# A hybrid decoder layer on one core: first unit in three pieces, products of zeros ahead of it, six buffers for rows of x, two roots through ACT

## The chip, the cores and the metric

The kernel runs on one core of one Trainium2 chip. A core has TensorE (PE, matrix products; PEld is its weight load), VectorE (DVE), ScalarE (ACT), GpSimd (POOL) and SyncE (SP, which here only issues DMAs), and 16 DMA engines that all queues share. The metric is device time in microseconds (us), the median of several runs.

## The reference

One decoder layer (DEPTH = 1) on 256 tokens and 16 learned meta tokens, 2048 wide, in float32:

```python
h = _rmsnorm(h_res, norm_mix_g[l])
proj = h @ w_in[l]                       # q 1024 | k 256 | v 256 | u 1024
q = _rmsnorm(q, q_norm_g[l]); k = _rmsnorm(k, k_norm_g[l])
attn = _sliding_window_attention(q, k, v, attn_sinks[l])    # 16 heads, 4 KV heads, window 128
ssm = _s5_mixer(u, ...)                  # 64 groups x 16 channels, complex state of 64, GELU, GLU
mix = concatenate([_rmsnorm(attn, ...), _rmsnorm(ssm, ...)])
h_res = h_res + mix @ w_out[l]
h2 = _rmsnorm(h_res, norm_mlp_g[l])
h_res = h_res + jnp.square(jax.nn.relu(h2 @ w_up[l])) @ w_down[l]
return h_res[:, N_META:]
```

`_rmsnorm` divides each row by the root of its mean square plus 1e-6.

## The kernel before

Weights come in units of 512 KB: 4 k-tiles of 128 rows by 256 columns (`cols`) or 2 by 512 (`rows`). `run` lists all units in `self.plan`; `unit` issues loads ahead (`load`), prepares the next ones (`part`) and hands one over. Most weights are split into a rounded part `hi` (ACT) and the rest `lo` (DVE), and a product is made of three fast ones (`mm3`). The first two phases, u0 and k0 (`RAW = 2`, eight units), are *whole*: the raw weights go into full float32 products, each recorded as two PE instructions. The operand of these phases is x transposed (`xT`, laid out by the host with the meta tokens first), 4 tiles of 4 k-tiles by 272 tokens. Tile `c` is loaded beside unit `c` of u0 by `load_xT`, on SP's queue, and scaled by the norm's weight on ACT by `split_xT`, one k-tile at a time. `split_hT` makes the rounded pair `hTh`, `hTl` of it for the phases after. The order of the phases is u0, k0, v0, q0, u1, q1, u2, u3 (`ORDER`), then the output projection, the gate and the MLP. u0's products run over two halves of 128 columns, each over the unit's four k-tiles.

The norm's divisor per token is applied late: `load_x` brings the rows of x in six pieces (two halves of 128 tokens, of the next 128, and of the 16 meta tokens), into buffers `xn` that hold 3 at a time; `token_rstd` squares and sums them on ACT and calls `rsqrt`, which makes the inverse root by an integer trick and three Newton steps on DVE (12 small operations). The result is spread over the partitions by small products (`rb`) and multiplied into k, v and u. `k_norm` calls `rsqrt` again for the heads of k. These six loads, and that of the state-space matrices `bc`, are issued by SP just before the last unit of k0.

Beside the projections run two generators, attention (`att`) and state space (`ssm`). `step`, after each unit, feeds them while a planner's clocks for DVE and ACT are less than a lead (1.5 us at first) ahead of the planner's clock for PE. That clock starts at 5.7 us for the first unit (`split_xT`). A scheduler then orders each engine's queue by priority and its own timing; on the chip each queue runs in that order.

`constants` sets up small tables at the start: a tile of zeros (DVE; `WARM = 0` products use it), the identity, the masks `m8`, `gm`, `blk2`, slopes (POOL). The five large tiles of the state-space operators (`Vr`, `Vi`, `Wr`, `Wn`, `MT`, each 128 x 1024) are cleared by POOL in `ssm_in(0)`.

Of the kernel before, what the change touches and what calls it, by code (L numbers as in the profile page):

```python
# [8 lines left out]
F32 = mybir.dt.float32  # L9
F32R = mybir.dt.float32r  # L10
I32 = mybir.dt.int32
AF = mybir.ActivationFunctionType
ALU = mybir.AluOpType
AX = mybir.AxisListType
MULT, ADD, SUB, MAX, MIN = ALU.mult, ALU.add, ALU.subtract, ALU.max, ALU.min

P = 128
D = 2048
# [6 lines left out]
HD = 64  # L25
SW = 1024
FF = 8192
EPS = 1e-6
NKT = D // P
CT = 4  # L30
# [22 lines left out]
RAW = 2  # L53
XROWS = (3, 2, 6)
BC = 3
HALVES = 1
WARM = 0
PTV, PMV, AOV = (3,), False, True
LEAD = (1.5, 3.0, 6.0, 1.0, 6.0)
PRICE = (1.0, 1.2, 1.0)  # L60
# [42 lines left out]
class Trunk:  # L103
    def __init__(self, tc, ins, out, dbg=None):
        self.tc = tc
        self.nc = PacedCore(tc.nc)
        self.clock = self.nc.clock
        self.i = ins
        self.out = out
        self.dbg = dbg or {}  # L110
        self.ssm, self.att, self.evac = [], [], []
        self.spent = {}
        self.rows_x, self.squared = [], []
        self.norms = iter(())
        self.halves = 1
        self.share, self.lead = 0.5, 1.5
        self.late = None
        self.plan, self.raws, self.units, self.when = [], {}, {}, {}
        self.nd = self.ns = self.nu = 0
# [72 lines left out]
            return self.ms2.tile([P, 512], F32, tag="ms2", name=name[1:])  # L192
        return self.ms.tile([P, 512], F32, tag="ms", name=name)

    def rsqrt(self, pool, y, ss, n, name, rows=P):

        sh = list(ss.shape)
        v = pool.tile(sh, F32, tag="rs_v", name=f"rv_{name}")
        self.ts(v, ss, 1.0 / n, MULT, EPS, ADD)
        ti = pool.tile(sh, I32, tag="rs_i", name=f"ri_{name}")  # L200
        self.nc.vector.tensor_scalar(ti, v.bitcast(I32), 1, None, op0=ALU.logical_shift_right)
        self.nc.vector.tensor_scalar(y.bitcast(I32), ti, -1.0, 1597463007.0, op0=MULT, op1=ADD)
        t = pool.tile(sh, F32, tag="rs_t", name=f"rt_{name}")
        for _ in range(3):
            self.tt(t, y, y, MULT)
            self.stt(t, t, -0.5, v, MULT, MULT)
            self.stt(y, t, 1.5, y, ADD, MULT)

    def load(self):
        n = self.nd  # L210
        dram, k0, nk, c0, ncol, first, _, whole = self.plan[n]
        tag = ("hi", "lo", "raw")[n % 3] if whole else "raw"
        raw = self.ring.tile([P, nk, ncol], F32, tag=tag, bufs=3, name=f"raw{n}")
        m = nk // HALVES if n == 0 else nk
        for k in range(0, nk, m):
            if first:
                first(k, m)
            self.nc.sync.dma_start(out=raw[:, k:k + m, :], in_=dram[(k0 + k) * P:(k0 + k + m) * P, c0:c0 + ncol].rearrange("(k p) c -> p k c", p=P))
        self.raws[n] = raw
        self.nd += 1  # L220
# [111 lines left out]
    def constants(self):  # L332
        nc, c = self.nc, self.cst

        w = self.st.tile([P, D // 2], F32, tag="xn", bufs=3, name="zeros")[:, 0:256]
        nc.vector.memset(w, 0.0)
        wp = self.ps("warm")
        for _ in range(WARM):
            nc.tensor.matmul(wp[:, 0:256], lhsT=w[:, 0:P], rhs=w, start=True, stop=True)
        g = nc.gpsimd  # L340
        self.ones = c.tile([P, 1], F32, name="ones")
        g.memset(self.ones, 1.0)

        nc.scalar.activation(c.tile([P, 1], F32, name="early"), self.ones, AF.Copy)
        self.ident = c.tile([P, P], F32, name="ident")
        make_identity(nc, self.ident)
        m8 = c.tile([P, 8], F32, name="m8")
        g.memset(m8, 1.0)
        g.affine_select(out=m8, in_=m8, pattern=[[-16, 8]], compare_op=ALU.is_ge, fill=0.0, base=0, channel_multiplier=1)
        g.affine_select(out=m8, in_=m8, pattern=[[16, 8]], compare_op=ALU.is_ge, fill=0.0, base=15, channel_multiplier=-1)  # L350
        self.m8 = m8
        self.gm = c.tile([P, 2], F32, name="gm")
        nc.vector.tensor_reduce(out=self.gm, in_=m8.rearrange("p (k x) -> p x k", x=2), axis=AX.X, op=ADD)
        self.blk2 = c.tile([P, 2], F32, name="blk2")
        nc.vector.tensor_reduce(out=self.blk2, in_=m8.rearrange("p (x k) -> p x k", x=2), axis=AX.X, op=ADD)
        self.slope = c.tile([P, 2, NH], F32, name="slope")
        self.qsc = c.tile([P, NH], F32, name="qsc")
        for h in range(NH):
            g.memset(self.slope[:, :, h:h + 1], -SLOPES[h])
            g.memset(self.qsc[:, h:h + 1], HD ** -0.5 / SLOPES[h])  # L360
# [39 lines left out]
    def load_xT(self, c, k, m):  # L400

        if k == 0:
            self.xT[c] = self.st.tile([P, 4, L], F32, tag="xT", bufs=4, name=f"xT{c}")
        r = 512 * c + P * k
        self.nc.sync.dma_start(out=self.xT[c][:, k:k + m, :], in_=self.i["xT"][r:r + P * m, :].rearrange("(k p) t -> p k t", p=P))

    def split_xT(self, c):

        t = self.xT[c]
        for k in range(4):  # L410
            kt = 4 * c + k
            self.nc.scalar.activation(t[:, k, :], t[:, k, :], AF.Copy, scale=self.g_in[:, kt:kt + 1])
        self.clock["t"] = max(self.clock["t"], 5.7 + 3.7 * c)

    def split_hT(self, c):
        for k in range(2):
# [4 lines left out]

    def load_x(self, n):

        k, h = n // 2, n % 2
        src = self.i["meta_tokens"] if k == 2 else self.i["x"][0][k * P:k * P + P, :]
        t = self.st.tile([P, D // 2], F32, tag="xn", bufs=3, name=f"x{k}{h}")[0:src.shape[0], :]
        self.nc.sync.dma_start(out=t, in_=src[:, h * (D // 2):(h + 1) * (D // 2)])
        self.rows_x.append(t)

    def token_rstd(self):  # L430

        nc = self.nc
        s2 = self.cst.tile([P, 3, 2], F32, name="s2x")
        ss = self.cst.tile([P, 3], F32, name="ss")
        nc.gpsimd.memset(s2, 1.0)
        for n in range(6):
            while n >= len(self.rows_x):
                yield
            t = self.rows_x[n]
            nc.scalar.activation(t, t, AF.Square, accum_out=s2[0:t.shape[0], n // 2, n % 2:n % 2 + 1])  # L440
            self.squared.append(n)
            yield
        nc.vector.tensor_reduce(out=ss, in_=s2, axis=AX.X, op=ADD)
        self.rs_x = self.cst.tile([P, 3], F32, name="rs_x")
        self.rsqrt(self.cst, self.rs_x, ss, D, "x")
        yield
        self.rb = self.asm.tile([P, L], F32, name="rb")
        rp = self.ps("rb")
        for k, (n, o) in enumerate(((P, NM), (P, NM + P), (NM, 0))):
            rr = self.KT[:, k, 0:P]  # L450
            nc.vector.tensor_copy(rr, self.rs_x[:, k:k + 1].to_broadcast([P, P]))
            nc.tensor.matmul(rp[:, o:o + n], lhsT=rr[0:n, :], rhs=self.ident[0:n, 0:n], start=True, stop=True)
        nc.vector.tensor_copy(self.rb, rp[:, 0:L])
        yield
# [172 lines left out]
    def ssm_in(self, Q):  # L627

        nc = self.nc
        if Q == 0:  # L630
            nc.gpsimd.tensor_scalar(self.C[1], self.C[1], -1.0, None, op0=MULT)
        if Q == 0:
            self.ops = [self.spb.tile([P, 8, CT, 2, 16], F32, name=nm) for nm in ("Vr", "Vi", "Wr", "Wn")]
            self.MT = self.spb.tile([P, 8, P], F32, name="MT")
            for z in self.ops + [self.MT]:
                nc.gpsimd.memset(z, 0.0)
        Vr, Vi = self.ops[0:2]
        (br, bi) = self.B
        yield from self.prod(Q, Vr, br, bi, self.Fr, self.Fi, SUB)
        yield from self.prod(Q, Vi, br, bi, self.Fi, self.Fr, ADD)  # L640
# [218 lines left out]
    def k_norm(self, kr):  # L859
        nc = self.nc  # L860
        NT, TW = 4, 68
# [5 lines left out]
        sp = self.ps("kss").rearrange("p (k n) -> p k n", n=4)  # L867
# [1 line left out]
            for i in range(2):  # L869
                nc.tensor.matmul(sp[0:TW, t, 2 * i:2 * i + 2], lhsT=sq[i][:, t * TW:t * TW + TW], rhs=self.blk2, start=True, stop=True)  # L870
        rk = self.atp.tile([TW, NT, 4], F32, name="rk")
        self.rsqrt(self.atp, rk, sp[0:TW, 0:NT, :], HD, "k")
        yield
        rbs = [self.ps(f"krb{i}")[:, 0:L] for i in range(2)]
        for t in range(NT):
# [203 lines left out]
    def run(self):  # L1079
# [22 lines left out]
        self.Vm = self.asm.tile([P, 2, 4, HD], F32, name="Vm")  # L1102
        self.qT = self.asm.tile([P, 8, NX], F32, name="qT")
        self.U = self.spd.tile([P, NPAIR, NCH], F32, name="U")
        self.grp, self.xT, self.ready = {}, {}, set()
        w_in, w_glu, w_out, w_up, w_down = (i[n][0] for n in ("w_in", "w_glu", "w_out", "w_up", "w_down"))
        tk = [slice(NM, NM + P), slice(NM + P, NM + 2 * P)]
        xt = [slice(0, P), slice(P, 2 * P)]

        self.cols(w_in, 1536, NKT, [lambda k, m, c=c: self.load_xT(c, k, m) for c in range(4)], [lambda c=c: self.split_xT(c) for c in range(4)], True)  # L1110
        loads = {BC: lambda k, m: nc.sync.dma_start(out=self.bc, in_=i["ssm_bc"])}
        for n in range(6):
            k = XROWS[0] + (n >= XROWS[2]) * (n - XROWS[2] + 1)
# [227 lines left out]
```

## Time and profile before

| | |
|---|---|
| median of 3 runs | 1065.33 us (1064.19 to 1066.98) |
| profiled run | 1063.85 us, its span 1062.1 us |
| PE busy | 1043.9 us, 98% of the span |
| DVE, ACT, POOL busy | 677.0, 517.8, 10.3 us |
| DMA | 192.07 MB, mean 181 GB/s |
| first product on PE | 7.22 us after the span's start |

A row of the timeline gives start, duration, engine, line, operation, tiles (out<-in), shapes and count (xN: N of them merged) and, in brackets, the idle time before it and what ended it. SPq rows are issues of DMAs. A row of waits gives the total, the count and the longest. Since all operations pass through helpers, most lines read L80 or L81; the tiles' names tell the place.

### The profile page before, as it was taken

Reading aid. Unit: us, or ns where it says so; the run is one execution under the profiler, and the core shown is the slowest. Engines: PE = TensorE matmul, PEld = TensorE weight load, DVE = VectorE, ACT = ScalarE, POOL = GpSimd, SP = SyncE. Lnnn points to the kernel's source line nnn. Section 1 sums busy time; section 2 is a strip of 40 time slices with the busy share of each in tenths; the row PEclk is TensorE's granted clock in tenths of the full one; section 3 lists DMA queues with packets and bytes.
Section 4 is the critical chain, followed back from the end, with each engine's and each line's share of the span. In section 5 each row is a group of like instructions: output and inputs, shape, how many; then the busy total and the mean of one; then the engine's idle time right before and its main releaser. Section 6 shows DMA issues by size and latency. Waiting matters only on the chain.

```text
span 1062.1 us, 14956 instructions
## 1 busy us (share of the span) xinstructions
PE 1043.9 (98%) x5724; PEld 896.5 (84%) x5724; DVE 677.0 (64%) x1121; ACT 517.8 (49%) x742; POOL 10.3 (1%) x62
## 2 busy tenths in 40 slices
PE   7999999999999999999999999999999999999998
PEld 5879788878998888888888888888888888888886
DVE  8988887739586766554556655456565555665553
ACT  6744768454475645433344543335444334544332
POOL 3000000000000000000000000000000000000000
PEclk9999999999999999999999999999999999999999
DMA  9563534155565666666666666666665666666673
GB/s 332 164 180 101 168 100 128 43 168 176 177 191 172 184 190 185 191 197 190 191 194 184 193 192 193 192 198 184 193 192 186 196 195 186 194 192 184 216 212 127
DMA packets 145929, 192.07 MB, mean 181 GB/s; under 512 B 9632, under 2 KB 97824, under 8 KB 145472
## 3 DMA queue, kind: packets, MB, share of 16 engines
q1 hardware_dynamic: 145856, 191.10, 58.3%
q8 instruction: 45, 0.74, 0.3%
q14 instruction: 28, 0.23, 0.1%
HBM read 186.03 MB, written 4.26 MB: 179 GB/s over the span
## 4 chain that ended last, share of the span: by engine, by line
PE 92%; DVE 4%; ACT 2%; issue 1%; DMA 1%; SPq 0%; ACTq 0%; DVEq 0%
PE up L81 34%; PE dn L81 33%; PE wb L81 4%; PE q L81 4%; PE u L81 4%; PE wt L81 3%; PE y L80 2%; PE g L81 2%; PE pv L80 2%; PE s L80 1%; DVE room L81 1%; PE z L80 1%; DVE gt L81 1%; DVE lo L80 1%; DMA xT<-in_xT 1%
## 5 line engine op out<-in xcount | busy, mean ns | idle before, releaser
L80 DVE TENSOR_TENSOR lo<-raw,hi 128x1024 fp32r<-128x1024 f32 x328 | 401.3, 1224 | 291.0 <-ACT hi L80 290.5
L80 ACT ACTIVATE hi<-raw 128x1024 fp32r<-128x1024 f32 x328 | 347.5, 1060 | 378.2 <-PE dn L81 199.5
L81 PE MATMUL up<-h,hi 128*128 128x512 f32 x1024 | 245.5, 391 | 0.0
L81 PEld LDWEIGHTS up<-h,hi 128*128 128x128 f32 x1024 | 188.0, 188 | 36.3
L81 PE MATMUL dn<-lo,ah 128*128 128x512 f32 x512 | 199.2, 389 | 0.0
L81 PE MATMUL dn<-hi,al 128*128 128x512 f32 x512 | 199.2, 389 | 0.0
L81 PE MATMUL dn<-hi,ah 128*128 128x512 f32 x512 | 178.4, 389 | 0.0
L81 PEld LDWEIGHTS up<-h,lo 128*128 128x128 f32 x1024 | 131.5, 191 | 5.1
L81 PE MATMUL up<-h,lo 128*128 128x256 f32 x1024 | 133.2, 283 | 0.0
L81 PEld LDWEIGHTS dn<-hi,ah 128*128 128x128 f32 x512 | 96.1, 188 | 20.0
L81 PEld LDWEIGHTS dn<-lo,ah 128*128 128x128 f32 x512 | 96.1, 188 | 19.9
L81 PEld LDWEIGHTS dn<-hi,al 128*128 128x128 f32 x512 | 96.1, 188 | 19.9
L81 ACT ACTIVATE r<-up 128x256 f32<-128x256 f32 x64 | 23.9, 373 | 56.4 <-PE up L81 56.4
L81 DVE TENSOR_TENSOR r<-up,r 128x256 f32<-128x256 f32 x64 | 27.0, 421 | 29.3 <-ACT r L81 29.3
L81 PE MATMUL wt<-hi,ma 128*128 128x512 f32 x128 | 40.5, 395 | 1.5 <-ACT ma L81 1.4
L81 PEld LDWEIGHTS wt<-hi,ma 128*128 128x128 f32 x128 | 23.7, 188 | 7.0 <-ACT ma L81 1.8
L81 PE MATMUL u<-hTh,lo 128*128 128x272 f32 x96 | 28.7, 301 | 0.0
L81 PE MATMUL u<-hTh,hi 128*128 128x272 f32 x96 | 28.5, 299 | 0.0
L81 PE MATMUL u<-hTl,hi 128*128 128x272 f32 x96 | 28.2, 294 | 0.0
L81 ACT ACTIVATE ah<-s 128x512 fp32r<-128x512 f32 x32 | 20.2, 630 | 15.2 <-DVE s L81 15.2
L81 PE MATMUL q<-lo,hTh 128*128 128x512 f32 x64 | 26.0, 407 | 0.8 <-DVE lo L80 0.8
L81 PE MATMUL wt<-lo,ma 128*128 128x512 f32 x64 | 25.1, 395 | 0.9 <-DVE lo L80 0.9
(289 smaller groups left out, 1161.8 us busy)
## 6 DMA issues: line engine op xcount, KB each, us to landing
raw<-in_w_up SPq DMA_DIRECT2D x128, 512.0 KB, 3.9
raw<-in_w_down SPq DMA_DIRECT2D x128, 512.0 KB, 4.1
raw<-in_w_in SPq DMA_DIRECT2D x40, 512.0 KB, 4.1
raw<-in_w_out SPq DMA_DIRECT2D x32, 512.0 KB, 4.0
raw<-in_w_glu SPq DMA_DIRECT2D x8, 512.0 KB, 4.3
xT<-in_xT SPq DMA_DIRECT2D x4, 544.0 KB, 7.4
x<-in_x SPq DMA_DIRECT2D x4, 512.0 KB, 10.2
xm<-in_x SPq DMA_DIRECT2D x2, 1024.0 KB, 6.2
```

Source lines behind the costliest of these rows:

```text
L80: return f(*args, **kw)
L81: return f(*args, **kw)
```

## The change

- `FIRST = ((0, 1), (1, 1), (2, 2))`: unit 0's weights and its `xT` tile are loaded in three pieces, of one, one and two k-tiles. The weights' pieces stay on SP's queue; those of `xT` tile 0 go to ACT's queue, ahead of ACT's first operation.
- `WARM = 4`: PE first multiplies zeros, four products of 256 columns.
- The buffers `xn` become six; the rows of the meta tokens are loaded first. The scratch for dynamic DMAs is set to 2048 bytes.
- `rsqrt` gets a second form for x and k: ACT's Sqrt (on the mean plus epsilon), DVE's reciprocal and one Newton step. ACT's first operation becomes a Sqrt.
- The five large tiles are cleared at the start, four by POOL and `Vr` by DVE; the two reductions of `m8` into `gm` and `blk2` move from the start to `ssm_in(0)`.
- The planner's PE clock starts at 4.0 instead of 5.7 us.

```diff
-HALVES = 1
-WARM = 0
+FIRST = ((0, 1), (1, 1), (2, 2))
+WARM = 4
...
-    def rsqrt(self, pool, y, ss, n, name, rows=P):
+    def rsqrt(self, pool, y, ss, n, name, table=False):
...
+        t = pool.tile(sh, F32, tag="rs_t", name=f"rt_{name}")
+        if table:
+            self.nc.scalar.activation(t, ss, AF.Sqrt, scale=1.0 / n, bias=self.eps[0:sh[0], :])
         self.ts(v, ss, 1.0 / n, MULT, EPS, ADD)
-        ti = pool.tile(sh, I32, tag="rs_i", name=f"ri_{name}")
...
-        for _ in range(3):
+        if table:
+            self.nc.vector.reciprocal(y, t)
+        else:
+            ti = pool.tile(sh, I32, tag="rs_i", name=f"ri_{name}")
...
+        for _ in range(1 if table else 3):
...
-        m = nk // HALVES if n == 0 else nk
-        for k in range(0, nk, m):
+        for k, m in FIRST if n == 0 else ((0, nk),):
...
-        w = self.st.tile([P, D // 2], F32, tag="xn", bufs=3, name="zeros")[:, 0:256]
+        w = self.st.tile([P, D // 2], F32, tag="xn", bufs=6, name="zeros")[:, 0:256]
...
-        nc.scalar.activation(c.tile([P, 1], F32, name="early"), self.ones, AF.Copy)
+        self.eps = c.tile([P, 1], F32, name="eps")
+        g.memset(self.eps, EPS)
+
+        self.ops = [self.spb.tile([P, 8, CT, 2, 16], F32, name=nm) for nm in ("Vr", "Vi", "Wr", "Wn")]
+        self.MT = self.spb.tile([P, 8, P], F32, name="MT")
+        nc.vector.memset(self.ops[0], 0.0)
+        for z in self.ops[1:] + [self.MT]:
+            g.memset(z, 0.0)
+        for k, m in FIRST:
+            self.load_xT(0, k, m)
+
+        nc.scalar.activation(c.tile([P, 1], F32, name="early"), self.ones, AF.Sqrt)
...
-        nc.vector.tensor_reduce(out=self.gm, in_=m8.rearrange("p (k x) -> p x k", x=2), axis=AX.X, op=ADD)
...
-        self.nc.sync.dma_start(out=self.xT[c][:, k:k + m, :], in_=...)
+        (self.nc.sync if c else self.nc.scalar).dma_start(out=self.xT[c][:, k:k + m, :], in_=...)
...
-        self.clock["t"] = max(self.clock["t"], 5.7 + 3.7 * c)
+        self.clock["t"] = max(self.clock["t"], 4.0 + 3.7 * c)
...
-        k, h = n // 2, n % 2
+        k, h = (n // 2 + 2) % 3, n % 2
...
-        self.rsqrt(self.cst, self.rs_x, ss, D, "x")
+        self.rsqrt(self.cst, self.rs_x, ss, D, "x", True)
...
-            for z in self.ops + [self.MT]:
-                nc.gpsimd.memset(z, 0.0)
+            nc.vector.tensor_reduce(out=self.gm, ...)
+            nc.vector.tensor_reduce(out=self.blk2, ...)
...
-        self.rsqrt(self.atp, rk, sp[0:TW, 0:NT, :], HD, "k")
+        self.rsqrt(self.atp, rk, sp[0:TW, 0:NT, :], HD, "k", True)
...
-    nc = bacc.Bacc("TRN2", target_bir_lowering=False, num_devices=1)
+    nc = bacc.Bacc("TRN2", target_bir_lowering=False, num_devices=1, dynamic_dma_scratch_size=2048)
```

More of the change, by code (lines that the diff above doesn't have):

```diff
@@ L112, in __init__ @@
         self.spent = {}
-        self.rows_x, self.squared = [], []
+        self.rows_x, self.squared, self.xT = [], [], {}
         self.norms = iter(())
@@ L193, in ps @@
         return self.ms.tile([P, 512], F32, tag="ms", name=name)
-    def rsqrt(self, pool, y, ss, n, name, rows=P):
+    def rsqrt(self, pool, y, ss, n, name, table=False):
         sh = list(ss.shape)
         v = pool.tile(sh, F32, tag="rs_v", name=f"rv_{name}")
+        t = pool.tile(sh, F32, tag="rs_t", name=f"rt_{name}")
+        if table:
+            self.nc.scalar.activation(t, ss, AF.Sqrt, scale=1.0 / n, bias=self.eps[0:sh[0], :])
         self.ts(v, ss, 1.0 / n, MULT, EPS, ADD)
-        ti = pool.tile(sh, I32, tag="rs_i", name=f"ri_{name}")
-        self.nc.vector.tensor_scalar(ti, v.bitcast(I32), 1, None, op0=ALU.logical_shift_right)
-        self.nc.vector.tensor_scalar(y.bitcast(I32), ti, -1.0, 1597463007.0, op0=MULT, op1=ADD)
-        t = pool.tile(sh, F32, tag="rs_t", name=f"rt_{name}")
-        for _ in range(3):
+        if table:
+            self.nc.vector.reciprocal(y, t)
+        else:
+            ti = pool.tile(sh, I32, tag="rs_i", name=f"ri_{name}")
+            self.nc.vector.tensor_scalar(ti, v.bitcast(I32), 1, None, op0=ALU.logical_shift_right)
+            self.nc.vector.tensor_scalar(y.bitcast(I32), ti, -1.0, 1597463007.0, op0=MULT, op1=ADD)
+        for _ in range(1 if table else 3):
             self.tt(t, y, y, MULT)
@@ L352, in constants @@
         self.gm = c.tile([P, 2], F32, name="gm")
-        nc.vector.tensor_reduce(out=self.gm, in_=m8.rearrange("p (k x) -> p x k", x=2), axis=AX.X, op=ADD)
         self.blk2 = c.tile([P, 2], F32, name="blk2")
-        nc.vector.tensor_reduce(out=self.blk2, in_=m8.rearrange("p (x k) -> p x k", x=2), axis=AX.X, op=ADD)
         self.slope = c.tile([P, 2, NH], F32, name="slope")
@@ L404, in load_xT @@
         r = 512 * c + P * k
-        self.nc.sync.dma_start(out=self.xT[c][:, k:k + m, :], in_=self.i["xT"][r:r + P * m, :].rearrange("(k p) t -> p k t", p=P))
+        (self.nc.sync if c else self.nc.scalar).dma_start(out=self.xT[c][:, k:k + m, :], in_=self.i["xT"][r:r + P * m, :].rearrange("(k p) t -> p k t", p=P))
     def split_xT(self, c):
@@ L422, in load_x @@
     def load_x(self, n):
-        k, h = n // 2, n % 2
+        k, h = (n // 2 + 2) % 3, n % 2
         src = self.i["meta_tokens"] if k == 2 else self.i["x"][0][k * P:k * P + P, :]
-        t = self.st.tile([P, D // 2], F32, tag="xn", bufs=3, name=f"x{k}{h}")[0:src.shape[0], :]
+        t = self.st.tile([P, D // 2], F32, tag="xn", bufs=6, name=f"x{k}{h}")[0:src.shape[0], :]
         self.nc.sync.dma_start(out=t, in_=src[:, h * (D // 2):(h + 1) * (D // 2)])
@@ L439, in token_rstd @@
             t = self.rows_x[n]
-            nc.scalar.activation(t, t, AF.Square, accum_out=s2[0:t.shape[0], n // 2, n % 2:n % 2 + 1])
+            nc.scalar.activation(t, t, AF.Square, accum_out=s2[0:t.shape[0], (n // 2 + 2) % 3, n % 2:n % 2 + 1])
             self.squared.append(n)
@@ L632, in ssm_in @@
         if Q == 0:
-            self.ops = [self.spb.tile([P, 8, CT, 2, 16], F32, name=nm) for nm in ("Vr", "Vi", "Wr", "Wn")]
-            self.MT = self.spb.tile([P, 8, P], F32, name="MT")
-            for z in self.ops + [self.MT]:
-                nc.gpsimd.memset(z, 0.0)
+            nc.vector.tensor_reduce(out=self.gm, in_=self.m8.rearrange("p (k x) -> p x k", x=2), axis=AX.X, op=ADD)
+            nc.vector.tensor_reduce(out=self.blk2, in_=self.m8.rearrange("p (x k) -> p x k", x=2), axis=AX.X, op=ADD)
         Vr, Vi = self.ops[0:2]
@@ L1104, in run @@
         self.U = self.spd.tile([P, NPAIR, NCH], F32, name="U")
-        self.grp, self.xT, self.ready = {}, {}, set()
+        self.grp, self.ready = {}, set()
         w_in, w_glu, w_out, w_up, w_down = (i[n][0] for n in ("w_in", "w_glu", "w_out", "w_up", "w_down"))
@@ L1108, in run @@
         xt = [slice(0, P), slice(P, 2 * P)]
-        self.cols(w_in, 1536, NKT, [lambda k, m, c=c: self.load_xT(c, k, m) for c in range(4)], [lambda c=c: self.split_xT(c) for c in range(4)], True)
+        self.cols(w_in, 1536, NKT, [None] + [lambda k, m, c=c: self.load_xT(c, k, m) for c in range(1, 4)], [lambda c=c: self.split_xT(c) for c in range(4)], True)
         loads = {BC: lambda k, m: nc.sync.dma_start(out=self.bc, in_=i["ssm_bc"])}
```

## The prediction

> **What bounds the kernel now.** I read the page first (engine totals), then PE's waits, then the work by stage, then the chain and the timeline where the change acts.
>
> ```profile
> PE 1043.9 (98%) x5724; PEld 896.5 (84%) x5724; DVE 677.0 (64%) x1121; ACT 517.8 (49%) x742; POOL 10.3 (1%) x62
> ```
> ```profile
> PE u L81 <- DMA raw<-in_w_in: 7.2, 1, 7.2
> PE kss L80 <- ACT ksq L81: 1.4, 1, 1.4
> PE wt L81 <- ACT ma L81: 1.4, 1, 1.4
> PE wt L81 <- DVE lo L80: 0.9, 1, 0.9
> PE z L80 <- DMA U<-du: 0.9, 1, 0.9
> PE q L81 <- DVE lo L80: 0.8, 1, 0.8
> PE v L81 <- ACT qT L81: 0.6, 1, 0.6
> PE vti L80 <- ACT VTr L81: 0.5, 1, 0.5
> ```
>
> PE is the bound: 98% of the span, and its waits add up to 13.7 us, 7.2 of them before its first product. A microsecond saved ahead of a stage in which PE never waits is kept to the end. The stages (stretch, its length, busy time of PE, PEld, DVE, ACT, POOL; last columns clock, DMA share, GB/s):
>
> ```profile
> 7.00:24.30 17.30, 17.08 (x65) 13.84 (x66) 16.93 (x106) 11.20 (x24) 2.88 (x11) 1.00 1.09 367
> 24.30:32.00 7.70, 7.70 (x35) 6.41 (x34) 7.56 (x32) 5.17 (x10) 0.84 (x1) 1.00 1.04 364
> 40.00:65.00 25.00, 21.61 (x162) 19.16 (x162) 24.14 (x66) 14.10 (x25) 0.00 (x0) 1.00 0.50 142
> 90.00:210.00 120.00, 120.00 (x862) 104.70 (x860) 96.59 (x254) 77.25 (x181) 0.23 (x2) 1.00 0.38 113
> ```
>
> So PE decides, except that from 7 to 65 us DVE is full as well, and 40 to 65 is where PE waits for DVE and ACT. Whatever PE gains at the front must be followed by DVE there, or the wait at 64 grows.
>
> **1. The first unit.** Now it is one transfer of x^T (544 KB) and one of weights (512 KB), behind the vectors (101 KB), all from SP.
>
> ```profile
> raw<-in_w_in SPq DMA_DIRECT2D x40, 512.0 KB, 4.1
> ...
> xT<-in_xT SPq DMA_DIRECT2D x4, 544.0 KB, 7.4
> ...
> vecs<-in_vecs SPq DMA_DIRECT2D x1, 101.0 KB, 2.1
> ```
> ```profile
> 0.92 0.27 DVE L81 MEMSET zeros<- 128x256 f32 x1 [0.92 <-PEq L1331]
> ...
> 1.25 0.42 SPq L405 DMA_DIRECT2D xT<-in_xT  x1
> ...
> 5.65 1.76 ACT L81 ACTIVATE xT<-xT,vecs 128x272 f32<-128x272 f32 x4 [3.36 <-DMA xT<-in_xT]
> ...
> 8.25 2.48 PE L81 MATMUL u<-xT,raw 128*128 128x272 f32 x5
> 11.43 2.03 PE L81 MATMUL u<-xT,raw 128*128 128x272 f32 x7
> 15.82 4.52 PE L81 MATMUL u<-xT,raw 128*128 128x272 f32 x19
> 24.30 8.41 PE L81 MATMUL k<-xT,raw 128*128 128x272 f32 x36
> ```
> ```profile
> L81 PE MATMUL u<-xT,raw x64: 392/392/791, 7.2 to 24.1; 128*128 128x272 f32 x64
> ```
> ```profile
> 0.00:3.00 3.00, 0.00 (x0) 0.00 (x0) 0.62 (x5) 1.49 (x2) 2.37 (x46) 1.00 0.32 57
> 3.00:4.00 1.00, 0.00 (x0) 0.00 (x0) 1.00 (x5) 0.00 (x0) 1.00 (x2) 1.00 0.95 306
> 4.00:5.00 1.00, 0.00 (x0) 0.00 (x0) 1.00 (x5) 0.00 (x0) 1.00 (x2) 1.00 1.06 360
> 5.00:6.00 1.00, 0.00 (x0) 0.00 (x0) 1.00 (x5) 0.35 (x1) 1.00 (x2) 1.00 1.10 386
> ```
>
> Early products start some 0.45 us apart (the five of the row from 8.25 less a last one of 0.65: 1.83 over four steps); later ones 0.229 ((4.52 - 0.39) / 18). The fast spacing sets in at about 11.4, so PE runs at half pace for its first 4.2 us, though the granted clock reads 1.00. The 64 instructions of u0 take 24.3 - 7.2 = 17.1 us; at 0.229 they would take 14.7.
>
> After: four products of zeros, two instructions each, 256 columns: 8 x 0.45 x 256/272 = 3.4 us from about 1.25 (the zeros are cleared by 1.19; PE's queue runs in order, so they are in the way until they end) to 4.7. The first two pieces (x^T 136 KB and weights 128 KB each) can be there by then: with the vectors 629 KB, which the four window rows pass at 4.5 us, less 0.45 for the issue of x^T that leaves SP's queue; ACT's scaling is 0.5 us a piece (1.76 for four, overlapped). The third piece holds half the unit. All 1157 KB (1.18 MB) had moved at 5.9 us by these rows (0.17 + 0.31 + 0.36 + 0.39), the weights had landed at 7.2, 1.3 later. With 0.45 saved the third piece lands near 6.8. So: k-tiles 0 and 1 from 4.7 to about 5.9, a pause to 6.8, tiles 2 and 3 to 7.75 (ACT's pace), the second half of the columns 4 x 0.45 = 1.8 to 9.55, three more units of 16 x 0.229 = 3.66: u0 ends at 20.55 instead of 24.3. Gain 3.75. ACT gives up some 1.2 us for three issues (0.4 each, by SP's rows), before it has anything to scale. Bounds: all in time, 4.7 + 14.7 = 19.4, gain 4.9; nothing sooner and no clock, gain 0.
>
> "TensorE: Matmul & The Clock Gate" of the Trainium skill (Part 1, What's actually happening) says that full clock follows a busy window of 3.4 us which runs freely, so 3.4 to 6.8 us after the first product. The 4.2 us here agree; by the late end (estimate from that page) full clock would come at 8.1 and the gain would be 1.4 us smaller. "DMA: Bandwidth & Descriptors" (Issuing engines are not separate DMA queues) says a second issuing queue saves only issue time; that is how I counted it, and were the two queues to share bandwidth unluckily the third piece would land at 7.2 as before and cost 0.4 of the gain.
>
> **2. Clearing moves.** Four operators go from POOL at 2.9 us to POOL at its start, the fifth to DVE.
>
> ```profile
> 2.88 0.96 POOL L636 MEMSET Vr<- 128x1024 f32 x1
> 6.44 0.95 POOL L636 MEMSET MT<- 128x1024 f32 x1
> 2.88 4.54 DVE L81 TENSOR_SCALAR vecs<-vecs 128x16 f32<-128x16 f32 x1 [0.61 <-DMA vecs<-in_vecs]
> 7.47 0.23 DVE L81 TENSOR_SCALAR room<-vecs 128x32 f32<-128x32 f32 x1
> ```
>
> DVE's first operation lasts exactly as long as POOL's five clears (2.88 to 7.39): it is held by them, and DVE really begins at 7.47. After, four clears of 0.89 from about 0.85 end at 4.4; POOL's small work that stood before them (2.1 of the 2.37 us up to 3.0) follows, to 6.5. DVE's own clear (about 1.1, four times the 0.27 for 256 columns) falls into time in which it has nothing. DVE begins between 4.4 and 6.5: 1 to 3 us sooner; I take 1.5, since many small POOL operations follow the long ones. The two reductions of m8, moved later, cost DVE about 0.2.
>
> **3. Six buffers for the rows of x.**
>
> ```profile
> SPq L427 <- ACT x L81: 6.9, 3, 4.2
> ```
> ```profile
> DVE ss L81 <- ACT x L81: 0.8, 1, 0.8
> ```
> ```profile
> L81 ACT ACTIVATE x<-x x6: 1042/1057/1057, 24.9 to 41.4; 128x1024 f32<-128x1024 f32 x4, 16x1024 f32<-16x1024 f32 x2
> ```
> ```profile
> bc<-in_ssm_bc SPq DMA_DIRECT2D x1, 1024.0 KB, 10.0
> ```
>
> With three buffers SP's queue waited 6.9 us for squares. Now all six go in a row, ahead of the last weights of k0. The squares (1.06 + 0.19 each) reach from 24.9 to 42.6, up to where PE's waits of 0.5 and 0.6 stand on ACT (VTr, qT); they can move into ACT's idle time of 7 to 32 us (17.3 - 11.20 + 7.7 - 5.17 = 8.6); DVE's wait of 0.8 goes. PE arrives 3.75 sooner, so I count 0.6 of the 1.1 (bounds 0 and 1.1). Price: k0's last weights stand behind 101 + 4 x 1056 + 3 x 512 + 1024 + 2176 KB, with their own 512 KB 9.8 MB: 1.22 by 6 us, the rest at 365 GB/s, is 29.5, landed 30.8. PE needs them at 20.55 + 3 x 3.66 = 31.5. It just fits; I take 0.2 (bounds 0 and 1.5).
>
> **4. Roots.** Twelve small DVE operations become five, for x and for k.
>
> ```profile
> L81 DVE SCALAR_TENSOR_TENSOR rs_x<-rt_x,rs_x x3: 142/145/155, 47.4 to 55.4; 128x3 f32<-128x3 f32 x3
> ```
>
> Seven fewer at about 0.1 us of queue time each (0.145 long, and such operations overlap): 0.7 for x. k's lie behind the wait for ksq and are covered by q's products; without that cover they would be worth the same again. The last of x's steps stands at 55.4, 13 us after the last square, because each waits its turn between other work; five turns and one hop to ACT should be over sooner. ACT loads a table before its first operation in either kernel, and k's root comes before the first exponential and the first Gelu, so no load is added.
>
> **5. The wait at 61 to 64 (0.8 + 1.4).** DVE must reach the products with rb sooner by as much as PE does (3.75 + 0.6 - 0.2 = 4.15). It has 1.5 (clears) + 0.8 (wait) + 0.7 - 0.2 (roots, reductions) = 2.8, and the planner's PE clock for the first unit falls from 5.7 to 4.0, so up to 1.7 us less state-space work is put ahead: 4.5. I leave the wait as it is: 0 (bounds: 2.2 worse, 2.2 better).
>
> **Sum.** 3.75 + 0.6 - 0.2 + 0 = 4.15, say 4.2 us. The profiled run took 1063.85 (span 1062.1 and 1.75 around it); the median of the three runs, 1065.33, is 1.5 above. Against the median: 1061.1.
>
> **Rivals.**
> *DVE follows only half way.* POOL's whole start holds it to 6.5 and the planner's shift does not help: 2.3 (1.0 + 0.8 + 0.5) where 4.15 are needed, the wait at 64 grows by 1.9, gain 2.3: 1063.0. For it: DVE's 24.14 of 25 busy. Against: ACT's and SP's waits go too.
> *The zeros come late.* If POOL's clears hold DVE's clear of the zeros as they hold the 4.54 us operation, the zero products run from 4.5 to 7.9, real ones follow, fast from 8.7 (two of 64 done by then): u0 ends near 22.9, gain 1.4: 1063.9. Against: "SBUF — State Buffer" (Who interferes with whom) of the Trainium skill exempts a DVE operation with at most one SBUF input outside the two-port modes; no row here shows a clear beside a long one.
> *Slower: the state-space tail comes out of its cover.*
>
> ```profile
> 279.33 2.82 PE wt L81 x12
> 282.15 6.56 PE g L81 x55
> ```
>
> These are rows of the chain: only 2.8 us of products separate the last y, which ends at 279.3, from g, which needs its results through two transfers. Less state-space work early (the planner's 1.7) shifts it later; once the tail is over 4.2 us later against PE, PE's idle time there exceeds the gain; at 8 us the time is 1065.3 - 4.2 + 8 = 1069. Against: DVE has 23 us free from 90 to 210.
>
> **How the numbers follow.** Forecast (gain 3.2 and more) 0.62; DVE half way 0.18; zeros late or nothing sooner 0.12; slower 0.08. 0.3% is 3.2 us, about what a measurement of this kernel can tell from no change: faster 0.62, within 0.3% 0.30, slower 0.08. Best case 4.9 + 1.1 + 2.2 = 8.2; the forecast's own range is 1057.1 to 1062.1. The range takes in the two small gains, the second down to 0.3 us: 1057.0 to 1065.0; slower is left out.
>
> **What would show it.** Right: zero products from 1.3, real ones from 4.7, k0 at about 20.5 instead of 24.30; DVE's first long operation over by 4.4 to 6.5; no SP wait on squares; the root of x before 50; q's wait for ksq not above 1.4. Wrong: first real product after 7, spacing of 0.45 beyond 9 us, waits at 60 to 65 above 4, or a gap between y and g at 270 to 280.

## The result, and the profile after

The changed kernel takes 1057.43 us (median of 4 runs, 1056.99 to 1058.02), the kernel before 1064.76 on the same chip: a ratio of 0.993 (95% interval 0.9918 to 0.9942). The profiled run took 1057.23 us with a span of 1055.5, against 1063.85 and 1062.1. So 6.6 us went out of the span, where 4.2 were forecast; the medians differ by 7.3, and 1057.43 lies 0.4 above the lower end of the predicted range.

The page's engine totals and PE's waits over the whole span, changed kernel (total, count, longest):

```profile
PE 1045.0 (99%) x5732; PEld 897.0 (85%) x5732; DVE 671.6 (64%) x1108; ACT 519.4 (49%) x744; POOL 10.6 (1%) x62
```
```profile
PE wt L81 <- DVE lo L80: 1.5, 1, 1.5
PE wt L81 <- ACT ma L81: 1.4, 1, 1.4
PE warm L81 <- DVE zeros L81: 1.2, 1, 1.2
PE u L81 <- ACT xT L81: 0.7, 1, 0.7
PE v L81 <- ACT hi L80: 0.6, 1, 0.6
PE u L81 <- DMA raw<-in_w_in: 0.2, 1, 0.2
```

PE is still the bound. Of the waits between 40 and 65 us (vti, v, q, kss: 3.4 us together) none is left; one has come at the start of v, 0.65 us on the timeline:

```profile
37.69 0.39 PE L81 MATMUL v<-hTh,hi 128*128 128x272 f32 x1 [0.65 <-ACT hi L80]
```

The two at wt, 2.3 us before, are now 2.9. Front of the timeline on PE:

```profile
1.25 3.78 PE L81 MATMUL warm<-zeros 128*128 128x256 f32 x8 [1.25 <-DVE zeros L81]
4.82 2.39 PE L81 MATMUL u<-xT,raw 128*128 128x272 f32 x8
7.46 2.07 PE L81 MATMUL u<-xT,raw 128*128 128x272 f32 x8 [0.25 <-DMA raw<-in_w_in]
10.27 11.24 PE L81 MATMUL u<-xT,raw 128*128 128x272 f32 x48 [0.73 <-ACT xT L81]
21.34 4.97 PE L81 MATMUL k<-xT,raw 128*128 128x272 f32 x21
```

The zero products end as the first piece is ready, the real ones run at full pace from the start, and k0 begins at 21.34 instead of 24.30. The DVE timeline, changed kernel, shows the other half:

```profile
1.35 0.91 DVE L81 MEMSET Vr<- 128x1024 f32 x1 [0.16 <-issue]
...
3.55 0.99 DVE L81 TENSOR_SCALAR vecs<-vecs 128x32 f32<-128x32 f32 x1
...
4.58 0.19 DVE L81 TENSOR_SCALAR room<-vecs 128x32 f32<-128x32 f32 x1
```

DVE's state-space work (`room`) starts at 4.58 instead of 7.47. Work by stage from 40 to 65 us, changed kernel (PE, PEld, DVE, ACT, POOL; clock, DMA share, GB/s): PE is busy all 25 us where it had 21.61.

```profile
40.00:65.00 25.00, 25.00 (x196) 23.09 (x195) 25.00 (x63) 13.79 (x22) 0.00 (x0) 1.00 0.63 179
```

To compare kernels whose state-space products sit in different places, I use one figure: the time at which a stage starts on PE, less the usual spacing of every product that PE did before it (the median spacing of each tile and shape in the kernel before). It is PE's time beyond its products, from the start to there. Its change from column to column tells in which stage a kernel loses time; only differences are used, and each row is one execution.

| us beyond the products at the start of | k0 | u1 | wt | wb | end of span | time, ratio to before |
|---|---|---|---|---|---|---|
| before | 16.2 | 21.0 | 25.0 | 28.6 | 33.6 | |
| changed | 13.2 | 14.9 | 17.2 | 22.0 | 27.0 | 0.993 |
| before + clears moved | 15.6 | 16.5 | 19.0 | 21.9 | 26.9 | 0.9936 |
| before + buffers | 15.2 | 18.5 | 20.2 | 21.2 | 26.2 | 0.992 |
| before + front only | 13.5 | 24.0 | 25.7 | 27.6 | 32.6 | 0.998 |
| changed, clears put back | 13.3 | 18.0 | 20.2 | 24.5 | 29.5 | 0.9953 |
| changed, no zeros | 14.0 | 14.9 | 18.4 | 24.0 | 29.0 | 0.9946 |
| changed, one piece | 16.9 | 17.1 | 19.5 | 21.3 | 26.4 | 0.9925 |
| changed, old roots | 13.3 | 15.3 | 15.9 | 18.1 | 23.0 | 0.9899 |
| changed, old planner clock | 13.0 | 13.9 | 16.2 | 24.3 | 29.3 | 0.9931 |
| changed, three buffers | 13.5 | 13.9 | 14.5 | 17.0 | 22.0 | 0.9886 |
| three buffers, no zeros | 13.3 | 13.7 | 17.5 | 21.8 | 26.8 | 0.9934 |
| changed, u3 more urgent | 13.1 | 14.0 | 15.1 | 16.4 | 22.1 | 0.989 |
| three buffers, four pieces, old clock | 16.0 | 16.4 | 17.0 | 19.0 | 23.9 | 0.9896 |

By this figure the changed kernel gained 3.0 us up to k0, 3.1 from k0 to u1, 1.7 from u1 to wt, and lost 1.2 after it. Executions of one kernel differ by stretches of half clock, 1.7 us each (last section): the kernel before took 1063.4 to 1064.4 us in the seven of one series with a mean clock of 1.000 and 1064.9 to 1066.7 in the other eight, and the profiled executions of no zeros (1059.2, median 1058.03) and old clock (1059.6, median 1057.61) hold one and two such stretches between wt and wb.

### The profile page after: what moved, and what is told of

The parts are those of the page before. It is cut to its first block, busy times and chain, and to the rows that moved or that the text cites. A ratio compares the mean times of both kernels' runs of the same rounds, so it can differ in the third digit from the quotient of the medians.

```text
span 1055.5 us, 14955 instructions
## 1 busy us (share of the span) xinstructions
PE 1045.0 (99%) x5732; PEld 897.0 (85%) x5732; DVE 671.6 (64%) x1108; ACT 519.4 (49%) x744; POOL 10.6 (1%) x62
## 4 chain that ended last, share of the span: by engine, by line
PE 94%; ACT 2%; DMA 2%; SPq 1%; issue 1%; DVE 0%; ACTq 0%; DVEq 0%
PE up L81 34%; PE dn L81 33%; PE q L81 4%; PE wb L81 4%; PE u L81 4%; PE wt L81 3%; PE y L80 2%; PE pv L80 2%; PE g L81 1%; PE v L81 1%; PE z L80 1%; PE s L80 1%; DMA x<-in_meta_tokens 1%; PE kp L80 1%; SPq L222 1%
## 5 line engine op out<-in xcount | busy, mean ns | idle before, releaser
L81 ACT ACTIVATE r<-up 128x256 f32<-128x256 f32 x64 | 23.9, 373 | 55.9 <-PE up L81 55.9
L81 PEld LDWEIGHTS wt<-hi,ma 128*128 128x128 f32 x128 | 23.7, 188 | 7.6 <-ACT ma L81 1.8
L81 PE MATMUL u<-hTh,lo 128*128 128x272 f32 x96 | 28.6, 298 | 0.0
L81 PE MATMUL u<-hTh,hi 128*128 128x272 f32 x96 | 28.6, 298 | 0.0
L81 ACT ACTIVATE ah<-s 128x512 fp32r<-128x512 f32 x32 | 20.2, 630 | 15.2 <-DVE s L81 15.2
L81 DVE SCALAR_TENSOR_TENSOR xm<-dn,rs_h,xm 128x512 f32<-128x512 f32 x32 | 22.5, 744 | 5.1 <-PE dn L81 5.1
```

The costliest lines, as they stand in the source:

```text
L81: return f(*args, **kw)
```

## The experiments

### The clears alone, and everything but the clears

```diff
# clears put back: the changed kernel, undone in constants and ssm_in(0)
-        nc.vector.memset(self.ops[0], 0.0)
-        for z in self.ops[1:] + [self.MT]:
-            g.memset(z, 0.0)
...
+            for z in self.ops + [self.MT]:
+                nc.gpsimd.memset(z, 0.0)
# clears moved: the kernel before, the same lines the other way
```

> The changed kernel with the five clears on POOL where they stood before, and the two reductions at the start. POOL's clears then hold DVE's first operation again, from about 3.4 to 7.4 (it was over at 4.54). Theory (DVE's supply decides from 8 to 65): DVE is 2.9 us later, PE's waits from 37 to 65 grow by 1 to 3 us, time 1058.5 to 1060.5. Rival: DVE's surplus is state-space work that can come later; PE's waits stay, time within 0.5 of 1057.4.

> The kernel before with one thing moved: the five clears go to the start of the program (Vr to DVE, the other four on POOL) and the two reductions of m8 to where the clears stood. First loads, buffers, roots and planner stay as before, and the order of TensorE's products around the first wt product is that of before, so the time can be read against before directly. Theory (DVE's early start removed the waits between 37 and 65 us): DVE's second tensor_scalar ends some 3 us sooner than before's 7.42 us although TensorE's first product still starts at about 7, the second group of u products starts 2 to 3 us sooner than before's 91.37 us, and the run gives 1061.5 to 1063 us where before gives 1064.8. Rival (the waits went because the first unit came sooner, or because of the buffers): the second group of u starts within 0.7 us of 91.37 and the run gives 1064 to 1065.

Clears put back: 1059.73 us (0.9953, interval 0.994 to 0.9965; the changed kernel 0.993). TensorE's order is the changed kernel's product for product. DVE's and PE's timeline, this kernel:

```profile
3.37 4.08 DVE L81 TENSOR_SCALAR vecs<-vecs 128x16 f32<-128x16 f32 x1 [1.07 <-DMA vecs<-in_vecs]
...
7.51 0.23 DVE L81 TENSOR_SCALAR room<-vecs 128x32 f32<-128x32 f32 x1
```
```profile
39.26 0.39 PE L81 MATMUL v<-hTh,hi 128*128 128x272 f32 x1 [2.08 <-ACT hi L80]
```

The hold is back, PE's wait ahead of v grows from 0.65 to 2.08 us, and at u1 PE is 3.1 us behind the changed kernel: 1.4 by that wait and 1.7 by the half clock that follows it (last section).

Clears moved, and nothing else: 1057.67 us (0.9936, 0.9923 to 0.9948), span 1055.5. That is the whole gain of the change, more than either theory had asked for. DVE's timeline and PE's only wait between 36 and 92 us:

```profile
2.82 0.76 DVE L81 TENSOR_SCALAR vecs<-vecs 128x16 f32<-128x16 f32 x1 [0.55 <-DMA vecs<-in_vecs]
...
3.64 0.89 DVE L81 TENSOR_SCALAR room<-vecs 128x32 f32<-128x32 f32 x1
```
```profile
PE kss L80 <- ACT ksq L81: 0.2, 1, 0.2
```

DVE's state-space work starts 3.2 us sooner (its first operation ends at 4.53, against 7.70), PE only 0.6 (k0 at 23.73), and 3.4 us of waits become 0.17. The other 1.5 us between u1 and wt show as no wait in either trace; PE's order differs there in part, and I can't name their cause.

### The front

```diff
# front only: before + FIRST, the ACT queue for xT tile 0, WARM = 4, the Sqrt as ACT's first
# no zeros: -WARM = 4   +WARM = 0
# one piece: -FIRST = ((0, 1), (1, 1), (2, 2))   +FIRST = ((0, 4),), xT tile 0 on SP's queue
```

> The kernel before with the front alone: three pieces, x^T's on ACT's queue, four products of zeros (and ACT's first operation as Sqrt); three buffers, old roots, clears and planner's clock as before. k0 starts near 21.3 instead of 24.3. Theory: nothing speeds DVE up, so PE's waits at 40 to 65 grow from 3.4 to 5.5 or 6.5 and the gain shrinks to 0 to 1 us: 1063.8 to 1064.8. Rival: the 3 us reach the end, near 1061.8.

> The changed kernel without the products of zeros. If they are worth what the prediction gave them (PE at full pace some 4 us sooner, half of it saved), u0 ends 1.5 to 2 us later than 21.34 and the time is near 1059.2. Rival: the first half of the unit then runs slowly from about 4.4 while the third piece is still on its way (it stopped PE until 7.46) and unit 1 is not scaled before 10.27 anyway, so the slow products fill time that PE spent waiting: k0 starts within 0.4 of 21.34 and the time is 1057.2 to 1057.9.

> The changed kernel with unit 0 in one transfer of x^T and one of weights, both from SP's queue as before; zeros, buffers, roots, clears as changed. If the pieces matter, the first product is back at 7.2 us, unit 0 takes 16 x 0.229 = 3.7 from there at full pace, ends at 10.9 instead of 9.5, and k0 starts at 7.2 + 14.7 = 21.9: 0.6 later than 21.34, time near 1058.0. If the idle time from 5.0 to 7.2 makes PE slow again, k0 starts near 24 and the time is near 1060. Rival: the second unit's scaling bounded both, nothing changes (within 0.3).

Front only: 1062.6 us (0.998, 0.9971 to 0.9989). k0 starts at 21.64, 2.7 us sooner than before, and at u1 PE is 3.0 us behind. PE's waits from 36 to 92 us, this kernel:

```profile
PE kss L80 <- ACT ksq L81: 3.1, 1, 3.1
PE rb L81 <- DVE KT L81: 1.9, 1, 1.9
PE v L81 <- ACT qT L81: 1.3, 1, 1.3
PE vti L80 <- ACT VTr L81: 0.9, 1, 0.9
```

7.2 us where before had 3.4: what PE wins, DVE has not done yet, and the win comes back as waits. From 63.1 to 69.9 us the clock is at half besides, which costs 2.3 us of products (last section). The 3.8 of waits and these 2.3 are about the 5.7 us by which this kernel falls behind before from k0 to u1. The total lies between the two forecasts.

No zeros: 1058.03 (0.9946, 0.9934 to 0.9958). Its front on PE:

```profile
4.60 17.66 PE L81 MATMUL u<-xT,raw 128*128 128x272 f32 x64 [4.60 <-DMA raw<-in_w_in]
22.09 4.29 PE L81 MATMUL k<-xT,raw 128*128 128x272 f32 x18
```

The products run slowly at first but never wait for a piece; k0 comes 0.75 us later, between the two forecasts, and at u1 both kernels stand at 14.9. So what the zeros win does not show at u1, where executions with the same queues differ by 1.0 us (next section). The difference in the table arises around wt, 1.7 of it by half clock in this execution.

One piece: 1055.87 (0.9925, 0.9913 to 0.9937).

```profile
7.38 17.85 PE L81 MATMUL u<-xT,raw 128*128 128x272 f32 x64 [2.35 <-ACT hTh L81]
25.06 1.31 PE L81 MATMUL k<-xT,raw 128*128 128x272 f32 x5
```

Zeros without early pieces buy nothing: PE idles 2.35 us behind them and the real products start slow again (17.85 us for 64; before, 17.1). k0 is 3.7 us later than in the changed kernel, 2.2 of it is left at u1. The total is below both forecasts and not above the changed kernel's, because of what happens around wt.

### Buffers, roots and the planner's clock

```diff
# three buffers: -tag="xn", bufs=6   +tag="xn", bufs=3
# buffers only: before + bufs=6, meta rows first, the scratch of 2048
# old roots: rsqrt(..., True) of x and k back to the old form
# old clock: -4.0 + 3.7 * c   +5.7 + 3.7 * c
```

> The changed kernel with three buffers for the rows of x. Theory: the waits of PE at 41 to 65 (3.4 us before, 0.65 after) went because the rows are squared sooner (last square at 33.7 instead of 42.6), so that x's root and rb are there before q0. Then some 2.5 us come back: rb's products after 52, a wait for ksq of over 1 us, time 1059.5 to 1060.5. Rival (DVE's earlier start did it, 3.40 instead of 7.47): the waits stay under 1.2 us and the time is within 0.6 of 1057.4.

> The kernel before with six buffers for the rows of x (meta rows first, scratch for dynamic DMAs of 2048 bytes) and nothing else. Theory: x's root starts some 8 us sooner, rb is ready before q0, and most of PE's waits at 41 to 65 (3.4 us) go: 2 to 2.8 us faster, 1062.0 to 1062.8. Rival (twelve steps and DVE's late start keep rb late): less than 0.7 us faster, over 1064.1.

> The changed kernel with the integer trick and three Newton steps for x and k. Theory: twelve steps that each wait their turn took 13 us in the kernel before, against 9 us for five now; rb comes some 4 to 5 us later (near 50 instead of 45.5), still before its users at 54 to 55 need it: 0 to 1 us, time 1057.4 to 1058.4. Rival (the roots' length was the wait at 64): rb after 55, wait for ksq back at 1.4 and more, time near 1059.7.

> The changed kernel with the planner's PE clock starting at 5.7 us again. Theory: 1.7 us more state-space work stands ahead of each product on DVE, so what q0 needs comes 1.7 later; since rb has some 7 us to spare now, at most 0.5 of it shows: 1057.0 to 1058.2. Rival: the planner's clock was a main part of the gain at 41 to 65: 1.7 us and more come back, time over 1059.

Three buffers: 1051.93 us (0.9886, 0.9872 to 0.9899). The waits between 36 and 92 us do not come back; even the one of 0.65 at v is gone, and at u1 this kernel stands at 13.9 where the changed one has 14.9. That does not show that six buffers cost 1.0 us, because old clock stands at 13.9 too.

Old clock: 1057.61 (0.9931, 0.9917 to 0.9944), as forecast, but not by the forecast's mechanism. The operations on PE, DVE and ACT stand in the changed kernel's order from first to last, so the planner's clock moved nothing. What differs by u1 is when DVE begins on `bc`, which a DMA brings. The changed kernel, then old clock:

```profile
24.52 0.69 DVE L81 TENSOR_TENSOR gt<-bc,Fr 128x512 f32<-128x512 f32 x1 [0.83 <-DMA bc<-in_ssm_bc]
```
```profile
23.51 0.69 DVE L81 TENSOR_TENSOR gt<-bc,Fr 128x512 f32<-128x512 f32 x1
```

The changed kernel with u3 more urgent (below) has the same queues up to 163 us, begins on `bc` at 23.62, has no wait at v and stands at 14.0 at u1. So 1.0 us at u1 is what two executions with the same queues differ by, and a smaller difference there tells nothing.

In the kernel before, alone, the buffers gain: 1056.38 (0.992, 0.9907 to 0.9934), 2.5 us at u1, the rest around wt. Old roots: 1053.42 (0.9899, 0.9884 to 0.9914). x's last step starts at 47.8 instead of 43.4 us; u1 is 0.4 behind, which is within that difference. Three buffers, buffers only and old roots lie 4 to 6 us below everything that was forecast for them.

### The order of the products around wt

Four of these versions (buffers only, one piece, old roots, four pieces below) are as fast as the changed kernel or faster although they are behind it at u1 (the first two within the intervals of the ratio). PE's order shows two patterns. In the kernel before, the changed one, and those without zeros, with the clears moved or put back and with the old clock, the last products of u3 (2, 10 or 18) stand directly ahead of wt, after the last y2 and kp products, and the first 16 products of z behind it stand in one block. In the others u3 is done 11 us or more before wt. The scheduler flips between these on small edits. Two runs test it.

```diff
# three buffers, no zeros: bufs=3 and WARM = 0 (its order around wt is that of the kernel before)
# u3 more urgent: the changed kernel, in the products of a phase
+            self.nc.tensor.ahead = self.sooner(100) if name == "u3" else None
```

> The changed kernel with three buffers for the rows of x and no products of zeros. Three buffers alone gave 1051.93 us, no zeros alone 1058.03. In this pair the products of TensorE before the first wt stand in the order of the kernel before: the last ten u3 products directly ahead of wt, z3's eight in one block. Theory (that order costs the 3 to 5 us by which the versions differ around wt): idle times ahead of wt's products wait for ACT and DVE again, the wt stage from its first product to the first g takes 56 us or more where three buffers alone took 54.3, and the run gives 1055.5 to 1058. Rival (three buffers themselves give the 5.5 us): the wt stage stays at 54.3 and the run gives 1051.9 to 1053.

> The changed kernel, with the products of u3 set 100 places higher in the scheduler's order of urgency and nothing else. Its products stand as in the changed kernel up to some 40 us ahead of the first wt; from there u3 comes earlier and is done before the last y2 and kp products. Theory (the place of the last u3 products costs the time around wt): the wt stage takes 53.3 to 54.5 us instead of 56.8, and the run gives 1052.5 to 1055 us. Rival (the place of u3 is a by-product of the real difference, which lies before): 1056.5 to 1058.5.

Three buffers without zeros: 1057.58 us (0.9934, 0.9922 to 0.9947). At u1 it is the best of all (13.7); its wt stage takes 56.8 us (218.40 to 275.19), with the waits below. Between u1 and wb it falls 5.0 us behind three buffers alone: 1.8 from wt on and 3.2 ahead of the first wt product, where the wait for `ma` explains 1.4 and no other shows.

```profile
PE wt L81 <- ACT ma L81: 1.4, 1, 1.4
PE wt L81 <- DVE lo L80: 1.3, 1, 1.3
PE z L80 <- ACT gh L81: 0.4, 1, 0.4
```

u3 more urgent: 1052.4 us (0.989, 0.9876 to 0.9903). All of PE's waits that the view of this kernel lists:

```profile
PE warm L81 <- DVE zeros L81: 1.2, 1, 1.2
PE u L81 <- ACT xT L81: 0.5, 1, 0.5
PE u L81 <- DMA raw<-in_w_in: 0.2, 1, 0.2
```

PE's order is the changed kernel's for the first 1031 instructions after the zeros, up to 163 us; some 410 more follow ahead of wt, in another order. Then wt waits for nothing and its stage takes 53.8 us instead of 56.8. Both runs went as the theory of the order said (this one 0.1 us below its range). The spans differ by 4.8 us, of which 0.9 stood at u1 already, where the order is the same; so the order is worth about 4 us in the changed kernel, more than half of the whole change. The edit moved others of those 410 too (attention's `at` and kp), so which of them frees wt is not told apart.

### A version with the best of each

```diff
# three buffers, four pieces, old clock
-FIRST = ((0, 1), (1, 1), (2, 2))
+FIRST = ((0, 1), (1, 1), (2, 1), (3, 1))
...
-tag="xn", bufs=6   -4.0 + 3.7 * c
+tag="xn", bufs=3   +5.7 + 3.7 * c
```

> The changed kernel with three buffers for the rows of x, the planner's first due time at 5.7 us as before, and the first unit in four pieces of one k-tile each. The order of TensorE's products is exactly that of three buffers alone (1051.93 us). Theory: the fourth piece takes the wait of 0.25 us for the third piece away, and the later due time lets DVE and ACT serve the u products first, worth up to 1 us by the second group of u as with six buffers; 1050.5 to 1052. Rival (with three buffers nothing waited there any more, and the extra piece delays the second unit by its issue of about 0.6 us): 1052 to 1053.

1053.81 us (0.9896, 0.9881 to 0.9912): a miss of both theories. PE's front, and work by stage (clock third from the end):

```profile
6.17 2.99 PE L81 MATMUL u<-xT,raw 128*128 128x272 f32 x12 [0.25 <-DMA raw<-in_w_in]
11.35 12.93 PE L81 MATMUL u<-xT,raw 128*128 128x272 f32 x48 [2.20 <-ACT xT L81]
24.11 2.23 PE L81 MATMUL k<-xT,raw 128*128 128x272 f32 x9
```
```profile
11.00:12.00 1.00, 0.65 (x2) 0.61 (x3) 0.18 (x2) 1.00 (x3) 0.00 (x0) 0.83 1.08 385
12.00:13.00 1.00, 1.00 (x3) 0.66 (x2) 0.73 (x2) 0.99 (x3) 0.00 (x0) 0.50 1.08 380
13.00:14.00 1.00, 1.00 (x4) 0.75 (x3) 1.00 (x6) 1.00 (x3) 0.00 (x0) 0.50 1.09 385
14.00:15.00 1.00, 1.00 (x4) 0.76 (x3) 1.00 (x12) 1.00 (x3) 0.00 (x0) 0.50 1.10 387
15.00:16.00 1.00, 1.00 (x6) 0.84 (x5) 1.00 (x7) 1.00 (x3) 0.00 (x0) 0.96 1.07 370
```

The second x^T tile is issued behind the extra piece, at 3.88 us instead of 2.66 (the changed kernel), PE waits 2.20 us for it instead of 0.73, and the clock then falls to half. Against three buffers alone the front gives 2.5 us back at k0, and 1.9 of that is left at the end. Three buffers alone remain the fastest kernel.

## Why the prediction was right, and where it was not

The sign and the size held (4.2 forecast, 6.6 in the spans), but the terms did not add up as written.

**Step 1, 3.75 at the front: measured 3.0.** The zeros ended at 4.82 (forecast 4.7) and the clock was up. The third piece let PE go on at 7.46 instead of 6.8, later still than the 7.2 of the step's last case, and what the step left out was the next tile: 0.73 us of wait for ACT's scaling of x^T tile 1. The slow start of the kernel before was read short: the spacing stays at 0.45 up to the product at 11.88, 4.7 us, not 4.2. Of the two halves of this step the pieces carry the gain; the zeros, for which most of the working was made, give 0.75 at k0 and nothing that shows at u1. The rival "zeros come late" fell: DVE's clear of the zeros took its 0.27 us and PE started at 1.25.

**Step 2, 1.5 us for DVE: 2.9.** Too careful: DVE's next operation came between the clears, not behind POOL's small work.

**Step 5 is the step that failed.** It left the waits of 40 to 65 us as they were, since DVE would come 4.5 sooner and PE 4.15. The waits fell by 2.75 (3.4 to 0.65). With the clears' 2.9 and the other terms as forecast the balance would read DVE 2.9 + 0.8 + 0.5 + 1.7 = 5.9, PE 3.0, so 2.9 in hand, but that agreement is luck: the 1.7 for the planner's clock is nothing (old clock has the same queues), and without it 1.2 is in hand. What the runs show is the direction: the clears alone take 3.2 us of waits away without the front, the front alone adds 3.8. Rival "DVE follows half way" was the right mechanism for the wrong kernel: with the clears in their old place it happens.

**What the other parts gain at the front does not reach the end.** Against the clears alone the changed kernel (front, buffers, roots and planner's clock on top) is 2.4 us ahead at k0, 1.6 at u1, 1.8 at wt and level at wb and at the end. A part is visible in the chain of waits. The longest run of wt products, clears alone and then changed:

```profile
248.17 17.78 PE wt L81 x78
```
```profile
246.52 18.25 PE wt L81 x78
```

A wt product takes 232 ns instead of 226 ((18.25 - 0.39) / 77 and (17.78 - 0.39) / 77): 1.1 us over 192. The kernel before has the shorter one as well (17.78 for 78). The longer one stands in all eleven versions with the new `eps` tile and ACT's first operation as Sqrt, the shorter in all three without; which of the parts that these eleven share is the cause was not tried. As a whole the wt stage is 0.7 us longer (56.8 against 56.1). The g stage takes the rest of the 1.8 (23.7 us against 22.6), of which waits explain 0.4; the remainder is open.

**Step 3, 0.6 - 0.2: 2.5 at u1** in the kernel before; on top of the rest no gain is shown (three buffers are at least as good). The last weights of k0 were in time, as worked out. **Step 4** has the last step of x's root at 43.4 instead of 55.4 (lines of `rs_x`, changed kernel); with old roots it stands at 47.8 and 0.4 is missing at u1, less than executions differ by.

```profile
L81 DVE SCALAR_TENSOR_TENSOR rs_x<-rt_x,rs_x x1: 154/154/154, 43.4 to 43.4; 128x3 f32<-128x3 f32 x1
```

**Slower by the state-space tail** did not happen: y ends at 272.2, g starts at 274.9, 2.7 us as before.

**Not foreseen at all** was that the order around wt is at stake in every small edit: about 4 us. By luck the kernel before and the changed one have the same poor order there, so it does not touch this result.

## What to carry to other kernels

- Before pricing a gain of the bound engine at the front, ask how much work its followers have done by then. Here the followers' start decided: moving five clears out of DVE's way gave as much as the whole change, the front without it 1 us of span.
- Where a scheduler sets the order, compare versions stage by stage and look at the order itself; an undo-one total can show a flip elsewhere (here 4 us and more) instead of the part undone.
- Test the parts alone as well as undone: the front alone is 3.0 us behind at u1, and the kernel with all parts is 1.6 ahead there of the one with the clears alone.
- Find out how far two executions with the same queues differ before a part is credited from one trace: here 1.0 us at u1 by the arrival of one load, and 1.7 by each stretch of half clock.

## What the runs showed of the hardware

**After a wait of 1.4 to 3.2 us on PE the clock can fall to half for 3.4 us or twice that.** The granted clock fell to 0.50 after waits of 2.08 us (clears put back), 2.20 (four pieces), 1.53 (no zeros), 1.38 and 1.58 (old clock). It did not after 1.38 and 1.52 (changed kernel, at wt). Old clock and the changed kernel have the same queues, so the length of the wait alone does not decide. In front only it fell 0.9 us into a wait of 3.15 us that followed one of 1.87, and stayed down twice as long, 6.8 us (0.81 over 60 to 65 us, 0.51 over 65 to 70). Added up over the rows above, the half clock of four pieces lasted 0.34 + 3 + 0.08 = 3.4 us. Old clock, behind the wait of 1.38 that ended at 217.16, gives 1.24 + 2.0 + 0.16 = 3.4:

```profile
218.00:220.00 2.00, 1.89 (x6) 1.24 (x5) 2.00 (x7) 1.26 (x3) 0.00 (x0) 0.69 0.99 410
220.00:222.00 2.00, 2.00 (x8) 1.60 (x7) 0.36 (x1) 0.00 (x0) 0.00 (x0) 0.50 1.01 336
222.00:224.00 2.00, 2.00 (x10) 1.62 (x9) 0.76 (x2) 1.84 (x3) 0.00 (x0) 0.96 0.98 394
```

Work by stage, clears put back, gives 1.12 + 2.0 + 0.32 = 3.4 as well. At half clock 3.4 us are 1.7 us of products lost:

```profile
40.00:42.00 2.00, 2.00 (x13) 1.81 (x13) 2.00 (x7) 2.00 (x4) 0.00 (x0) 0.72 0.14 37
42.00:44.00 2.00, 2.00 (x11) 2.00 (x10) 2.00 (x5) 1.80 (x4) 0.00 (x0) 0.50 0.73 232
44.00:46.00 2.00, 2.00 (x17) 2.00 (x16) 2.00 (x8) 0.48 (x1) 0.00 (x0) 0.92 0.84 251
```

The Trainium skill, "TensorE: Matmul & The Clock Gate" (Part 1, What's actually happening), gives a window of about 3.4 us for both directions. The time at half clock agrees; that waits of 1.38 to 2.20 us were enough does not, and the measurement decides.

**POOL's clears hold some DVE operations, not others.** DVE's own clear of Vr took 0.91 us in the middle of POOL's, while its `tensor_scalar` and what followed were held to the end of one clear (0.76 us, clears alone) or of all five (4.54 us before, 4.08 with the clears put back). "SBUF — State Buffer" of the Trainium skill (Who interferes with whom) exempts operations with at most one SBUF input outside the two-port modes, in which a `tensor_scalar` can run; the traces agree, though none shows in which mode the `tensor_scalar` ran. That one operation is held over five clears in one kernel and slips in between two in another, no run here explains.
